# Five gate blocks computed as seven products, early sums moved beside the attention, gates kept in DRAM

## The chip, the core and the metric

The kernel runs on one core of one Trainium2 chip, whose engines work side by side: TensorE (PE) multiplies matrices, VectorE (DVE) and ScalarE (ACT) do elementwise work, GpSimd (POOL) and SyncE (SP) mostly issue DMA transfers here. The metric is the time of one execution on the device in microseconds (us), as the median of several runs.

## What is computed

One layer of an encoder with 512 tokens and a width of 2048, all in float32:

```python
def reference(x, ...):                       # x: (1, 512, 2048)
    h = rmsnorm(x, norm_mix)
    proj = h @ w_in                          # 2048 x 8704
    qa, ka, va, qb, kb, vb, ga, gb = split(proj)
    out_a = window_attention(rope(rmsnorm(qa)), rope(rmsnorm(ka)), va, sink)
    out_b = neighbourhood_attention(rmsnorm(qb), rmsnorm(kb), vb, rpb)
    merged = (sigmoid(ga) * (out_a @ w_branch_a)
              + sigmoid(gb) * (out_b @ w_branch_b))
    x = x + merged @ w_out
    u = conv3(rmsnorm(x) @ w_up)             # up: 2048 x 11264, gate and value
    gate, val = split(u)
    return x + (silu(gate) * val) @ w_down   # down: 5632 x 2048
```

`ga` and `gb`, the gates, are 2048 wide each. The factors of h by rows (1/rms of a token) and by columns (norm_mix) are applied apart: the acts carry norm_mix, and results are multiplied by the row factor.

## The kernel before

Matrices are worked off in **units**: a unit is 1024 columns by 128 rows of weights, for instance two k-tiles of 128 rows by 512 columns (512 KB). Activations lie transposed, 128 features by 512 tokens in a tile. A float32 product is made of three matmuls, hi x hi, hi x lo and lo x hi: ACT casts the weights to a rounded `hi` (L155), DVE subtracts (`lo`, L156). A plain unit has 8 pairs of k-tile and output tile, so 24 matmuls of 512 columns each, all recorded at L78, the line of `mm`; all SP transfers are recorded at L75. `hi` and `lo` have two buffers each, the raw weights three.

In the order of the program the stages are: the projections with both attentions between them (72 units: k and v of A 8, q_a in two halves of 8, and for each of four pairs of heads of B 4 units of v_b and 8 of q_b and k_b; the attention of a pair runs behind the projections that follow), gate blocks 0 and 1, gate block 2 (called the third gate block below; the attention's pools are closed at its start), branch A (out_a @ w_branch_a in four blocks), gate block 3, four gate blocks of B, branch B, `out` (w_out in four blocks), `up` and `down`.

Only `up` and `down` are worked in **products**: by the scheme of Strassen and Winograd a 2 x 2 block product needs seven products instead of eight. The price is sums of weights and of activations. Of the weights, a unit has four sums (L574 of 512 elements, L577 and L578 of 256 each); those of the activations are made by `forms` (sums at L627 to L630, casts at L638, subtractions at L639). Casting the weights is L597, subtracting L598; the combination of the seven results stands at L743 to L760. A product unit is 42 matmuls of 256 columns.

For part of the units of `up`, the sums are made **early** and kept in DRAM (`make_early`): f is loaded, added and stored by GpSimd (L581) in four of five units between the third gate block and `out`, 76 in all; `up` then loads sums in place of adding.

The order of instructions within an engine is the Tile scheduler's. It starts from the order of the program; `keep` holds an instruction in program order. The queue of an engine runs strictly in that order. Lines which the steps use: heads are squared, reduced, normed and rotated (L303 to L328), transposed and split (L335, L228, L229); v is transposed at L384. In the attention scores get bias and mask (L504, L508), are reduced (L449), raised (L456), scaled (L466), transposed and split (L477, L481, L482). A gate leaves PSUM by a multiplication with the row factor (L785) and the sigmoid (L786). `split_parts` (L832, L833) splits the attention's outputs for the branches. `wst_ctx.close()` ends the pool of plain weights and opens the one of products ("w"), before in the last unit of `out`.

Of the kernel before, what the change touches and what calls it, by code (L numbers as in the profile page):

```python
# [11 lines left out]
F32 = mybir.dt.float32  # L12
F32R = mybir.dt.float32r
AF = mybir.ActivationFunctionType
ALU = mybir.AluOpType
# [24 lines left out]
def trunk_kernel(  # L40
# [24 lines left out]
    def slot(dt=F32):  # L65
        return big.tile([P, S], dt, tag="s", name="s", bufs=N_SLOTS)
# [48 lines left out]

    steps, units, queue = [], [], deque()
    at = {"load": 0, "sums": 0, "prep": 0, "use": 0}

    def step(layout, w, cols, acts, evac, k0=0, nk=KD, before=None, pre=None, post=None, rate=RATE):

        width = sum(n for _, n in cols)
        kpb = 1024 // width
        steps.append(partial(
            run_step, layout, kpb, width, nk, acts, evac, before, pre, post, rate))
        for k in range(0, nk, kpb):
            units.append(Plain(w, k0 + k, kpb, cols))

# [34 lines left out]
    def prep_to(n, between=(), **kw):  # L162

        for u in units[at["prep"]:n + 1]:
            if hasattr(u, "first") and u.first > ffn.get("limit", -1):
# [378 lines left out]

    ffn, products_, early, made = {}, [], deque(), deque()
    keep = tc.keep_in_program_order

    class Product:
# [10 lines left out]
        def ready(self, phase, n):  # L559
            return "f" in ffn and not early and self.first <= n  # L560

# [9 lines left out]
        def sums(self):  # L571
            if not self.made:
# [5 lines left out]
                keep(nc.vector.tensor_tensor(f[:, 6], f[:, 5], f[:, 1], ALU.add))  # L578

        def store(self):  # L580
            nc.gpsimd.dma_start(self.kept, self.f[:, 3:])  # L581
            self.made = True
# [20 lines left out]
    def make_early():  # L603


        if "f" not in ffn or not early:
            return
        made.append(0)
        if len(made) % 5 == 0:
            return  # L610
        n = len(made) - len(made) // 5 - 1
        for move, i in (("store", n - 2), ("sums", n - 1), ("load", n)):
            if 0 <= i < len(early):
                getattr(early[i], move)()
        if n - 2 == len(early) - 1:
            early.clear()

# [57 lines left out]
    class Tiles:  # L675


        def __init__(self, w, first):
            self.w, self.first = w, first

        def ready(self, phase, n):
            return "f" in ffn and not early and self.first <= n

# [7 lines left out]
        def prep(self, *between):  # L691
            hi, lo = (
                ffn["w"].tile(
                    [P, 1024 + 32], F32R, tag=f"{half}a{self.first % 2}",
                    name="w" + half, bufs=1)[:, 16:16 + 1024].rearrange(
                        "p (f n) -> p f n", f=4)
                for half in "hl")
            keep(nc.scalar.copy(hi, self.f))
            keep(nc.vector.tensor_tensor(lo, self.f, hi.bitcast(F32), ALU.subtract))
            self.hi, self.lo = (v.rearrange("p (b c) n -> p b (c n)", b=2) for v in (hi, lo))  # L700
            for work in between:
                work()

    def tiles_by_halves(w, pairs, acts, evac, before=None, after=None):
# [28 lines left out]
        for i in range(n):  # L733
            units.append(Tiles(w[pairs[i]], len(units)))
            products_.append(units[-1])
# [39 lines left out]

    ra, sg, merged, oa, ob = {}, {}, [None] * KD, [], []

    def gates(c0, base, evac, **kw):
        step("f", w_in, [(c0 + base * P, 512)], hT, lambda m, ps: evac(base + m, ps), **kw)

    def branch(w, m0, acts, evac, **kw):
        step("f", w, [(m0 * P, 512)], acts, lambda m, ps: evac(m0 + m, ps), nk=8, **kw)

    def sigmoid(m, ps, s):
# [3 lines left out]
    half = {}  # L788

    def slot_of(tag):  # L790

        if tag is None:
            return slot()
        if tag not in half:
            half[tag] = quad(tag)
            return half[tag][:, 0]
        return half.pop(tag)[:, 1]

    def gate_first(store):
        def evac(m, ps):  # L800
            tag = ({2: "u", 3: "o"} if store is sg else {2: "a"}).get(m // 4)
            store[m] = slot_of(tag)
            sigmoid(m, ps, store[m])
        return evac

    def gate_after(m, ps):
        s = scratch()
        sigmoid(m, ps, s)
        nc.vector.tensor_tensor(ra[m], ra[m], s, ALU.mult)

    def evac_a(m, ps):
        if m < 12:
            nc.vector.tensor_tensor(ra[m], ps, ra[m], ALU.mult)
        else:
            ra[m] = slot()
            nc.scalar.copy(ra[m], ps)

    def evac_b(m, ps):
        s, r = sg[m], ra[m]
        nc.vector.tensor_tensor(s, ps, s, ALU.mult)  # L820
        nc.vector.tensor_tensor(r, r, s, ALU.add)
        merged[m] = split(r)

# [10 lines left out]

    def split_out(dst, src):
        for o in src:
            dst.append(load_parts(o))
            split_parts(*dst[-1])

    for blk in range(2):  # L840
        gates(C_GA, blk * 4, gate_first(ra))

    def load_a():
        end_attention()
        oa.extend(load_parts(o) for o in out_a)

    def before_gate(kb):
        if kb >= 4:
            for parts in oa[2 * kb - 8:2 * kb - 6]:
                split_parts(*parts)  # L850

    gates(C_GA, 8, gate_first(ra), pre=load_a, before=before_gate)
    for blk in range(4):
        branch(w_branch_a, blk * 4, oa, evac_a)
    gates(C_GA, 12, gate_after)

    def before_b(kb):
        if kb >= 4:
            split_out(ob, out_b[2 * kb - 8:2 * kb - 6])
# [21 lines left out]
    def project_out(n):  # L881
# [5 lines left out]
        def before(kb):  # L887
# [5 lines left out]
            if n == 3 and kb in (2, 4, 6, 7):  # L893
                form_pair({2: 2, 4: 3, 6: 4, 7: 5}[kb])
            if n == 3 and kb == 7:
                wst_ctx.close()
                ffn["w"] = ctx.enter_context(tc.tile_pool(name="w", bufs=2, reuse_waits="tile"))
                ffn["limit"] = at["use"] + 1

# [6 lines left out]
        def post():  # L906
            if n == 3:
                ffn["limit"] = len(units)
                prep_to(at["use"] + 1)
                form_pair(6)  # L910
                form_pair(7)

        step("f", w_out, [(n * 512, 512)], merged, evac, pre=pre, before=before, post=post)

# [213 lines left out]
```

## Time and profile before

| | |
|---|---|
| median of 3 runs | 2505.21 us (2503.06 to 2506.1) |
| the profiled execution: its time | 2502.81 us |
| its span in the trace | 2501.0 us |
| attention and gate blocks 0 and 1 | 0 to 580 us |
| third gate block | 580 to 624 us |
| branches and other gates | 624 to 1017 us |
| `out` | 1017 to 1191 us |
| `up` | 1193 to 2030 us |
| `down` | 2030 to 2501 us |

How to read what follows: a row of instructions gives line, engine, operation, output <- input with shape and count, then the busy time and the mean ns of one, then the idle time of the engine just before them and what ended it. A row of stretches gives, for a stretch of the execution, the busy time of each engine. Busy PE is no proof that PE runs at its full pace, as matmuls overlap; the number of matmuls in a full stretch gives their pace.

### The profile page before, as it was taken

What the parts mean: (1) busy time and instruction counts of PE and PEld (TensorE: products, weight loads), DVE (VectorE), ACT (ScalarE), POOL (GpSimd) and SP (SyncE); (2) the same over time, 40 slices, a digit from 0 to 9 for tenths busy, and PEclk for the clock granted to TensorE, in tenths of its full rate; (3) what the DMA queues carried; (4) which work ended last, traced back from release to release, by engine and by line L of the source; (5) the groups of instructions that cost most, each with busy time, mean ns of one, the idle gap of its engine ahead of it and who ended that gap; (6) DMA issues with size and microseconds to landing.
All of it is one profiled execution on the core that took longest, in us unless ns stands there. A gap on an engine that the chain in (4) does not pass through costs nothing.

```text
span 2501.0 us, 43289 instructions
## 1 busy us (share of the span) xinstructions
PE 2471.2 (99%) x16726; PEld 2275.1 (91%) x16726; DVE 1763.1 (70%) x2643; ACT 1226.9 (49%) x1843; POOL 202.9 (8%) x234
## 2 busy tenths in 40 slices
PE   9999999999999999999999999999999999999998
PEld 7888888888888888888999999999999999999998
DVE  6566454644545457655788888888888878696897
ACT  5355544543222233233576666666666665453633
POOL 0100000000000000100011111111111101000000
PEclk9999999999999999999999999999999999999999
DMA  5322222337787887874488888888888897776753
GB/s 190 94 83 89 91 91 91 99 92 225 257 256 244 254 279 256 278 253 160 148 211 224 225 227 219 230 220 217 233 221 218 244 283 213 209 188 170 226 161 120
DMA packets 338064, 487.04 MB, mean 195 GB/s; under 512 B 27840, under 2 KB 251200, under 8 KB 337856
## 3 DMA queue, kind: packets, MB, share of 16 engines
q1 hardware_dynamic: 294912, 377.38, 48.7%
q0 software_dynamic: 38464, 98.49, 16.8%
q10 hardware_dynamic: 4480, 8.39, 0.9%
q8 instruction: 131, 2.15, 0.3%
q14 instruction: 77, 0.63, 0.1%
HBM read 354.22 MB, written 83.89 MB: 175 GB/s over the span
## 4 chain that ended last, share of the span: by engine, by line
PE 94%; DMA 2%; DVE 2%; ACT 1%; issue 0%; SPq 0%; DVEq 0%; ACTq 0%
PE mm L78 91%; PE tr L78 2%; DMA s<-act 1%; DMA f<-in_w_down 1%; PE tr L477 1%; DVE wl L598 1%; PE tr L335 0%; DVE s L970 0%; ACT wh L597 0%; SPq L75 0%; DVE t L743 0%; DVE u L1039 0%; PE tr L384 0%; ACT s L638 0%; DMA s<-in_x_t 0%
## 5 line engine op out<-in xcount | busy, mean ns | idle before, releaser
L78 PE MATMUL mm<-s,wh 128*128 128x256 f32 x7476 | 1245.9, 277 | 10.2 <-ACT wh L597 7.8
L78 PEld LDWEIGHTS mm<-s,wh 128*128 128x128 f32 x7476 | 1088.1, 188 | 11.8 <-ACT wh L597 9.0
L78 PE MATMUL mm<-s,wl 128*128 128x256 f32 x3738 | 939.4, 277 | 2.9 <-DVE wl L598 2.9
L78 PE MATMUL mm<-s,hi 128*128 128x512 f32 x2304 | 688.5, 390 | 0.9 <-DVE s L785 0.9
L597 ACT CAST wh<-f 128x1024 fp32r<-128x1024 f32 x486 | 446.5, 942 | 449.0 <-PE mm L78 315.6
L78 PEld LDWEIGHTS mm<-s,wl 128*128 128x128 f32 x3738 | 660.8, 188 | 3.7 <-DVE wl L598 3.6
L598 DVE TENSOR_TENSOR wl<-f,wh 128x1024 fp32r<-128x1024 f32 x486 | 517.1, 1088 | 144.2 <-ACT wh L597 143.8
L78 PEld LDWEIGHTS mm<-s,hi 128*128 128x128 f32 x2304 | 431.6, 188 | 89.3 <-ACT s L786 1.3
L156 DVE TENSOR_TENSOR lo<-raw,hi 128x1024 fp32r<-128x1024 f32 (+1 forms) x201 | 244.9, 1218 | 379.2 <-ACT hi L155 375.9
L155 ACT CAST hi<-raw 128x1024 fp32r<-128x1024 f32 (+1 forms) x201 | 210.6, 1048 | 537.9 <-PE mm L78 476.9
L78 PE MATMUL mm<-s,lo 128*128 128x512 f32 x1152 | 423.7, 390 | 0.0
L78 PE MATMUL mm<-hi,s 128*128 128x512 f32 x896 | 284.9, 394 | 5.4 <-ACT hi L155 5.4
L78 PEld LDWEIGHTS mm<-s,lo 128*128 128x128 f32 x1152 | 216.4, 188 | 44.1
L78 PEld LDWEIGHTS mm<-hi,s 128*128 128x128 f32 x896 | 167.7, 189 | 38.1 <-ACT hi L155 5.4
L78 PE MATMUL mm<-lo,s 128*128 128x512 f32 x448 | 176.2, 394 | 0.0
L574 DVE TENSOR_TENSOR f<-f 128x512 f32<-128x512 f32 x243 | 166.4, 685 | 0.0
L578 DVE TENSOR_TENSOR f<-f 128x256 f32<-128x256 f32 x243 | 103.2, 425 | 7.8
L577 DVE TENSOR_TENSOR f<-f 128x256 f32<-128x256 f32 x243 | 103.2, 425 | 7.7
L78 PEld LDWEIGHTS mm<-lo,s 128*128 128x128 f32 x448 | 84.6, 189 | 16.7
L939 POOL DMA_DIRECT2D o<-a x44 | 52.9, 1202 | 575.7 <-ACT a L938 430.9
L581 POOL DMA_DIRECT2D sums<-f x76 | 40.7, 535 | 571.7 <-DVE f L578 571.7
L936 ACT ACTIVATE o<-u,smalls 128x512 f32<-128x512 f32 x88 | 71.1, 808 | 9.9 <-DMA act<-o 7.0
(140 smaller groups left out, 1644.6 us busy)
## 6 DMA issues: line engine op xcount, KB each, us to landing
f<-in_w_up SPq DMA_DIRECT2D x252, 256.0 KB, 4.0
f<-in_w_up SPq DMA_DIRECT2D x428, 128.0 KB, 4.1
raw<-in_w_in SPq DMA_DIRECT2D x103, 512.0 KB, 3.9
o<-a POOLq DMA_DIRECT2D x88, 511.0 KB, 8.1
sums<-f POOLq DMA_DIRECT2D x76, 512.0 KB, 5.0
f<-sums SPq DMA_DIRECT2D x76, 512.0 KB, 5.2
s<-act SPq DMA_DIRECT2D x168, 128.0 KB, 3.9
f<-in_w_down SPq DMA_DIRECT2D x67, 256.0 KB, 3.3
```

The lines of the kernel that those rows point to most:

```text
L78: nc.tensor.matmul(o, l, r, start=start, stop=stop, skip_group_check=True)
L155: nc.scalar.copy(hi[:, c:c + n], self.raw[:, c:c + n])
L156: nc.vector.tensor_tensor(lo[:, c:c + n], self.raw[:, c:c + n], hi[:, c:c + n].bitcast(F32), ALU.subtract)
L477: nc.tensor.transpose(b[:, (j - j0) * P:(j - j0 + 1) * P], pr[j][:, off:off + P], ident)
L574: keep(nc.vector.tensor_tensor(f[:, 3:5], f[:, 2::-2], f[:, 6].unsqueeze(1).to_broadcast([P, 2, 256]), ALU.add))
L577: keep(nc.vector.tensor_tensor(f[:, 5], f[:, 4], f[:, 2], ALU.add))
L578: keep(nc.vector.tensor_tensor(f[:, 6], f[:, 5], f[:, 1], ALU.add))
L581: nc.gpsimd.dma_start(self.kept, self.f[:, 3:])
L597: keep(nc.scalar.copy(hi, f))
L598: keep(nc.vector.tensor_tensor(lo, f, hi.bitcast(F32), ALU.subtract))
L936: keep(nc.scalar.activation(self.o[:, m], u[:, m], AF.Identity, bias=cb[:, i:i + 1], scale=cw[:, i, 1:2]))
L939: keep(nc.gpsimd.dma_start(self.o[:, :, 1:], first[:, :, :S - 1], accum_op=ALU.add))
```

## The change

Gate blocks 3 to 7 (the last of A, the four of B) become products, eight units each. For that the activations h need sums too (`forms`, 56 tiles in slots): they are made in the third gate block, which stays plain. x is loaded once more from DRAM in pairs of tiles into `quad("a")`, which has two buffers, scaled by norm_mix on ACT, and summed, cast and subtracted. The pool of product weights is opened at the end of this block instead of at that of `out`.

All gates are computed ahead of the branches; the sigmoids of A and B are written to DRAM through GpSimd and loaded again two tiles at a time in the branches (`held`). Branches and `out` keep plain units, in the products' buffers (`Tiles`).

The early sums are no longer made in f buffers but in slots: of each unit's sums, 128 x 512 and 2 x 128 x 256, DVE makes the same three additions, at each unit from the tenth on in the attention and gate blocks 0 and 1 (77 groups), and 11 more in the branches, in quads. Per unit SP gets, in this order, two stores of the group added one unit before (256 KB each), then four loads of 128 KB.

```diff
+    def make_early():
-        made.append(0)
-        if len(made) % 5 == 0:
-            return
...
+        if added:
+            added.popleft().store()
+        if fetched:
+            fetched[0].add()
+            added.append(fetched.popleft())
+        if early and any(a <= at["use"] < b - 2 for a, b in windows):
+            early[0].fetch()
+            fetched.append(early.popleft())
...
+        def add(self):
+            a, b = self.early
+            c = quad("o")[:, 0] if "q" in ffn else slot()
+            c = c.rearrange("p (t n) -> p t n", t=2)
+            add = lambda *args: keep(nc.vector.tensor_tensor(*args, ALU.add))
+            add(c, a, b[:, 0].unsqueeze(1).to_broadcast([P, 2, 256]))
+            add(b[:, 0], c[:, 1], a[:, 0])
+            add(b[:, 1], b[:, 0], b[:, 1])
+            self.early = c, b
...
+        def store(self):
-            nc.gpsimd.dma_start(self.kept, self.f[:, 3:])
+            for i, o in enumerate(self.early):
+                dma(self.kept[:, 2 * i:2 * i + 2], o)
...
+    def load_x(j):
+        held[j] = quad("a")
+        dma(held[j], x_t[2 * j * P:(2 * j + 2) * P].rearrange("(a p) n -> p a n", p=P))
+    def form_h():
+        j = len(hf)
+        if j < KD // 2:
+            x = held.pop(j)
+            for i in range(2):
+                nc.scalar.activation(
+                    x[:, i], x[:, i], AF.Copy, scale=gmix[:, 2 * j + i:2 * j + i + 1])
+            hf.append(forms(x))
+            if j + 2 < KD // 2:
+                load_x(j + 2)
+    def before_forms(kb):
+        if kb != 6:
+            form_h()
+        if kb == 7:
+            wst_ctx.close()
+            ffn["w"] = ctx.enter_context(tc.tile_pool(name="w", bufs=2, reuse_waits="tile"))
...
     for blk in range(2):
-        gates(C_GA, blk * 4, gate_first(ra))
+        gates(blk * 4, gate_to_slot)
+    windows.append((9, len(units)))
+    gates(8, gate_to_quad, pre=pre_forms, before=before_forms, post=post_forms)
+    for blk in range(3, 8):
+        gate_products(
+            blk, kept=range(4) if blk == 3 else (1, 2),
+            before=parts_behind(out_a, oa, 1) if blk == 7 else None)
+    windows.append((len(units) + 2, len(units) + 64))
     for blk in range(4):
-        branch(w_branch_a, blk * 4, oa, evac_a)
-    gates(C_GA, 12, gate_after)
...
+        branch(w_branch_a, blk, oa, gate_a, evac_a, before=parts_behind(out_b, ob, 0))
     for blk in range(4):
-        gates(C_GB, blk * 4, gate_first(sg), before=before_b if blk == 3 else None)
-    for blk in range(4):
-        branch(w_branch_b, blk * 4, ob, evac_b)
+        branch(w_branch_b, blk, ob, gate_b, evac_b)
```

The new names of lines: casts and subtractions of plain weights are L162 and L163, the early additions L603, the scale of x L840, casts and subtractions of `forms` L665 and L666, its sums L654 to L657. Two places show how rows move.

First, the end of q_b and k_b of the third pair of heads, where the last four tiles are normed (`rq`, `qr`) while the attention of the pair of heads before ends (`pl`, `s`). DVE's queue there, before:

```order
L156 TENSOR_TENSOR lo_3747<-raw_3744,hi_3746 128x1024
L308 TENSOR_REDUCE rq_127<-t_3806 128x4
L229 TENSOR_TENSOR s_3676<-tr_3670,s_3675 128x512
L239 TENSOR_SCALAR rq_127<-rq_127 128x4
L482 TENSOR_TENSOR pl_3629<-tr_3625,ph_3628 128x256
L229 TENSOR_TENSOR s_3717<-tr_3711,s_3716 128x512
L313 TENSOR_TENSOR qr_3804<-qr_3804,rq_127 128x512
L308 TENSOR_REDUCE rq_127<-t_3813 128x4
```

and in the change, where `lo_4367` belongs to the first unit after it (v_b of the next pair), as `lo_3747` does above:

```order
L489 TENSOR_TENSOR pl_4215<-tr_4210,ph_4214 128x384
L320 TENSOR_TENSOR qr_4462<-qr_4462,rq_127 128x512
L236 TENSOR_TENSOR s_4284<-tr_4278,s_4283 128x512
L603 TENSOR_TENSOR s_4320<-s_4271,s_4272 128x512
L320 TENSOR_TENSOR qr_4469<-qr_4469,rq_127 128x512
L470 RECIPROCAL rc_4182<-sm_4145 128x4
L489 TENSOR_TENSOR pl_4225<-tr_4221,ph_4224 128x256
L603 TENSOR_TENSOR s_4272<-s_4320,s_4271 128x256
L236 TENSOR_TENSOR s_4337<-tr_4331,s_4336 128x512
L603 TENSOR_TENSOR s_4272<-s_4272 128x256
L163 TENSOR_TENSOR lo_4367<-raw_4364,hi_4366 128x1024
```

The three additions (L603) have come in, and `lo` of that unit, which stood ahead of the norms, has moved behind the last of them (`qr`) and behind the last subtraction of the tail. The same place in PE's queue, where the normed heads are transposed (`tr` from `qr`); before, between matmuls of the first two units behind (`hi_3746`, then `hi_3776` with `lo_3777`):

```order
L335 MATMUL tr_3936<-ident_91,qr_3811 128x2x4x16
L335 MATMUL tr_3984<-ident_91,qr_3811 128x2x4x16
L335 MATMUL tr_4024<-ident_91,qr_3811 128x2x4x16
L78 MATMUL mm_3833<-s_317,hi_3746 128x512
L78 MATMUL mm_3833<-s_316,lo_3747 128x512
L78 MATMUL mm_3832<-s_359,hi_3776 128x512
L78 MATMUL mm_3832<-s_360,hi_3776 128x512
L335 MATMUL tr_4064<-ident_91,qr_3804 128x2x4x16
L335 MATMUL tr_4064<-ident_91,qr_3811 128x2x4x16
L78 MATMUL mm_3832<-s_359,lo_3777 128x512
```

and in the change:

```order
L342 MATMUL tr_4792<-ident_91,qr_4448 128x2x4x16
L342 MATMUL tr_4792<-ident_91,qr_4455 128x2x4x16
L342 MATMUL tr_4792<-ident_91,qr_4462 128x2x4x16
L342 MATMUL tr_4792<-ident_91,qr_4469 128x2x4x16
L78 MATMUL mm_4476<-s_265,hi_4366 128x512
L78 MATMUL mm_4476<-s_266,hi_4366 128x512
```

All sixteen transposes, of which these are the last four, now stand ahead of the first matmul of the next unit.

Second, the third gate block. ACT's queue before held, after the eight casts of out_a, nothing but the next weights:

```order
L832 CAST s_5298<-s_5299 128x512
L832 CAST s_5301<-s_5302 128x512
L155 CAST hi_5310<-raw_5308 128x1024
L155 CAST hi_5344<-raw_5342 128x1024
L155 CAST hi_5381<-raw_5379 128x1024
```

In the change it holds, in one unit, the scales of a pair of x (`a_6396`) ahead of `hi`, and behind it the casts of the pair before (`a_6336`):

```order
L665 CAST s_6393<-a_6276 128x256
L665 CAST s_6435<-a_6336 128x256
L665 CAST s_6438<-a_6336 128x256
L840 ACTIVATE a_6396<-a_6396,gmix_86 128x512 x2
L162 CAST hi_6400<-raw_6398 128x1024
L665 CAST s_6441<-t_6431 128x256
L665 CAST s_6444<-t_6430 128x256
L665 CAST s_6447<-t_6430 128x256
L665 CAST s_6450<-t_6431 128x256
L665 CAST s_6453<-a_6336 128x256
```

DVE's queue in the change, for the same pair, with `lo` of the unit ahead of the sums (`t`):

```order
L163 TENSOR_TENSOR lo_6401<-raw_6398,hi_6400 128x1024
L654 TENSOR_TENSOR t_6430<-a_6336 128x512
L656 TENSOR_TENSOR t_6431<-t_6430,a_6336 128x256
L657 TENSOR_TENSOR t_6431<-t_6431,a_6336 128x256
L666 TENSOR_TENSOR s_6441<-t_6431,s_6441 128x256
L666 TENSOR_TENSOR s_6444<-t_6430,s_6444 128x256
L666 TENSOR_TENSOR s_6447<-t_6430,s_6447 128x256
L666 TENSOR_TENSOR s_6450<-t_6431,s_6450 128x256
L666 TENSOR_TENSOR s_6453<-a_6336,s_6453 128x256
```

and SP's queue, where each pair of x stands ahead of a unit's raw weights:

```order
L75 DMA a_6276<-in_x_t 128x2x512
L75 DMA raw_6278<-in_w_in 128x2x512
L75 DMA a_6336<-in_x_t 128x2x512
L75 DMA raw_6338<-in_w_in 128x2x512
L75 DMA a_6396<-in_x_t 128x2x512
L75 DMA raw_6398<-in_w_in 128x2x512
```

A pair takes the buffer of the pair but one before it: `a_6396` that of `a_6276`, whose last reader on DVE is the subtraction that writes `s_6393`. So three queues now carry the forms of h between the casts, subtractions and loads of the weights.

More of the change, by code (lines that the diff above doesn't have):

```diff
@@ L164, in prep_to @@
         for u in units[at["prep"]:n + 1]:
-            if hasattr(u, "first") and u.first > ffn.get("limit", -1):
+            if getattr(u, "first", -1) > ffn.get("limit", -1):
                 break
@@ L559, in ready @@
         def ready(self, phase, n):
-            return "f" in ffn and not early and self.first <= n
+            return "f" in ffn and self.first <= n
         def load(self):
@@ L681, in ready @@
         def ready(self, phase, n):
-            return "f" in ffn and not early and self.first <= n
+            return "f" in ffn and self.first <= n
         def load(self):
@@ L785, in sigmoid, with gates, gate @@
+    def gates(base, evac, **kw):
+        step("f", w_in, [(C_GA + base * P, 512)], hT, lambda m, ps: evac(base + m, ps), **kw)
+    def gate(m, ps, s):
         nc.vector.tensor_tensor(s, ps, rows["m"], ALU.mult)
         nc.scalar.activation(s, s, AF.Sigmoid)
[L788 to L804, printed above, removed]
@@ new lines, in parts_behind, with before, branch, before_unit @@
+    def parts_behind(src, dst, first):
+        def before(kb):
+            n = 2 * (kb - first)
+            if 0 <= n < 8:
+                dst.extend(load_parts(o) for o in src[n:n + 2])
+            for parts in dst[max(0, n - 2):max(0, n)]:
+                split_parts(*parts)
+        return before
+    def branch(w, blk, acts, gate_of, evac, before=None):
+        def before_unit(kb):
+            if before:
+                before(kb + 4 * blk - 8)
+            if kb == 1:
+                for j in range(2):
+                    held[j] = quad("a")
+                    dma(held[j], gate_of[2 * blk + j])
+        step("f", w, [(blk * 512, 512)], acts, lambda m, ps: evac(4 * blk + m, ps), nk=8,
+             before=before_unit, unit=Tiles)
@@ L894, in before @@
                 form_pair({2: 2, 4: 3, 6: 4, 7: 5}[kb])
[L895 to L898, printed above, removed]
         def evac(o, ps):
```

127 lines of the change are left out of this document (73 added, 54 removed).

## The prediction

> **What bounds the kernel now.** First the page's head and its chain of work that ended last, then the table of busy time by stretch, which shows each stage by itself (columns: stretch; length, then busy us and instructions of PE, of its weight loads, of DVE, ACT and POOL; granted clock; DMA share; GB/s).
>
> ```profile
> span 2501.0 us, 43289 instructions
> PE 2471.2 (99%) x16726; PEld 2275.1 (91%) x16726; DVE 1763.1 (70%) x2643; ACT 1226.9 (49%) x1843; POOL 202.9 (8%) x234
> PE 94%; DMA 2%; DVE 2%; ACT 1%; issue 0%; SPq 0%; DVEq 0%; ACTq 0%
> ...
> 170.00:180.00 10.00, 10.00 (x50) 8.68 (x49) 9.08 (x18) 6.61 (x10) 3.39 (x3) 1.00 0.17 52
> 180.00:190.00 10.00, 10.00 (x52) 8.39 (x51) 10.00 (x21) 2.87 (x5) 1.01 (x1) 1.00 0.31 97
> 200.00:300.00 100.00, 100.00 (x517) 86.12 (x516) 54.77 (x106) 51.32 (x108) 4.03 (x4) 1.00 0.28 89
> 580.00:624.00 44.00, 43.12 (x191) 35.69 (x191) 23.70 (x35) 14.18 (x20) 2.38 (x4) 1.00 0.68 213
> 755.00:930.00 175.00, 175.00 (x774) 144.91 (x773) 93.58 (x140) 48.16 (x57) 14.09 (x27) 1.00 0.80 256
> 1400.00:1700.00 300.00, 300.00 (x2635) 300.00 (x2634) 260.31 (x340) 195.98 (x254) 38.41 (x32) 1.00 0.85 225
> ```
>
> PE carries 94% of the chain and is full in nearly every stretch, so the time is PE's work plus the places where PE waits. Such places are few now. DVE's 55% at 200 to 300 us is a mean, though: at 180 to 190 us, where the heads of q_a are normed and rotated, DVE has nothing left (10.00 of 10.00). What is put on DVE in the attention must be judged there, not by the mean. The stretches also give PE's price: 175.00/774 = 0.226 us for a 512-wide matmul, 300.00/2635 = 0.114 us for a 256-wide one; one plain unit of 24 matmuls is 5.43 us.
>
> The waits show how far ahead weights are prepared:
>
> ```profile
> ACT hi L155 <- PE mm L78: 476.9, 137, 6.2
> PE mm L78 <- ACT wh L698: 2.5, 1, 2.5
> ```
>
> 137 times the cast of the next weights stood waiting for PE to release a buffer: the lead of the preparation is already used up, about one unit. A late DVE has some 5 us of cover and no more.
>
> **Term 1, PE's work.** Gate blocks 3 to 7 go from 192 matmuls of 512 columns each to 336 of 256. Removed: 5 x 192 x 0.226 = 217 us. Added: 5 x 336 x 0.114 = 191 us. Net **-26**. Their sums, casts and combinations are what `up` does already; at 1400 to 1700 us DVE needs 260 of 300 us beside a full PE, and that row is the cover. The last gate block also splits out_a; by my count of its instructions DVE has about 39 us there for 38 us of PE, at most 1 to 3 us.
>
> **Term 2, early sums beside the attention.** Rows of instructions (last figures: busy, mean ns of one):
>
> ```profile
> L574 DVE TENSOR_TENSOR f<-f 128x512 f32<-128x512 f32 x243 | 166.4, 685 | 0.0
> L578 DVE TENSOR_TENSOR f<-f 128x256 f32<-128x256 f32 x243 | 103.2, 425 | 7.8
> L577 DVE TENSOR_TENSOR f<-f 128x256 f32<-128x256 f32 x243 | 103.2, 425 | 7.7
> L156 DVE TENSOR_TENSOR lo<-raw,hi 128x1024 fp32r<-128x1024 f32 (+1 forms) x201 | 244.9, 1218 | 379.2 <-ACT hi L155 375.9
> ...
> L482 DVE TENSOR_TENSOR pl<-tr,ph 128x256 fp32r<-128x256 f32 (+1 forms) x64 | 30.3, 486 | 24.4 <-ACT ph L481 24.4
> L449 DVE TENSOR_REDUCE nm<-p 128x1 f32<-128x256 f32 (+1 forms) x64 | 29.0, 478 | 0.2
> L313 DVE TENSOR_TENSOR qr<-qr,rq 128x512 f32<-128x512 f32 (+1 forms) x28 | 18.1, 648 | 5.5 <-POOL rq L240 5.5
> L308 DVE TENSOR_REDUCE rq<-t 128x4 f32<-128x512 f32 (+1 forms) x28 | 17.8, 643 | 5.6 <-ACT t L306 5.6
> L508 DVE TENSOR_TENSOR p<-p,masks 128x256 f32<-128x256 f32 (+1 forms) x32 | 14.6, 484 | 0.0
> L504 DVE SCALAR_TENSOR_TENSOR p<-tr,bias 128x256 f32<-128x256 f32 (+1 forms) x32 | 14.4, 486 | 21.4 <-PE tr L78 11.9 <-DMA bias<-in_bias_b 9.3
> L229 DVE TENSOR_TENSOR s<-tr,s 128x512 fp32r<-128x512 f32 x18 | 11.9, 686 | 6.5 <-ACT s L228 6.4
> L239 DVE TENSOR_SCALAR rq<-rq 128x4 f32<-128x4 f32 (+1 forms) x28 | 4.4, 165 | 0.3
> ```
>
> 77 groups of three adds (0.685 + 2 x 0.425 = 1.535 us) make 118 us of new DVE work, each group kept in program order between two units' `lo`. The same sums leave later stages, where PE was full in any case, so that relief gains nothing. At 170 to 190 us DVE had 0.9 us free in 20, and about four groups (6.1 us) come in: at least 5 us must come out there.
>
> The order of the change tells more (section on the change): where a block of heads ends, no matmuls of projections are left between its transposes, and `lo` of the next unit stands behind the whole tail. Take the end of q_b and k_b of the third pair of heads. After the scores that `p_4158` needs, DVE has until `lo_4367`: three each of L504, L508 and L449 (4.3), two L308 and four L313 (3.9), four L482 (1.9), two L229 (1.4), four small ones (0.7), the three adds (1.5) and `lo` (1.2), in all 15.0 us. PE has, by width, 34 transposes of 128 (0.057 each, in proportion to 0.226 for 512), 9 matmuls of 384, 9 of 256 and 5 of 512, about 5.6 us, and two that need only `hi` (0.5). The gap is 15.0 - 6.1 = 8.9; some instructions overlap their neighbours a little, so I take 8. Counted likewise: 12.5 at the end of q_a's second half, 8 at the end of the fourth pair, 5.4 ahead of gate block 1, 4.4 and 2.7 around the first two pairs, 1.1 in q_a's first half; sum **42**. Bounds: with 0.08 us overlapped for each instruction 27, and 20 if matmuls fall between the transposes of one tail after all; above, if the losses chain through ACT, whose casts of the tail stand before the next `hi`, 55. I take **+38**, near the count by rows.
>
> SP's order changes too: per unit it now holds raw weights, two stores that wait for the adds of two units back, four fetches. The next raw load is queued behind a store that waits for DVE. Cover: that load is issued a unit ahead (5.4 us) and lands in 3.9 (row below). I add nothing; without the cover, 3.9 us at each of the six larger ones, 23, which the upper end holds. The rate rises by 1.05 MB in each unit, from 89 GB/s to about 250; at 755 to 930 us 256 GB/s went beside a PE busy for 175.00 of 175.00 us, so rate is not a limit.
>
> **Term 3, the third gate block, which now also forms h.** It took 44 us (580 to 624), 8 units at 5.43. The change puts a loop through four queues into each unit: x pair j+2 may be loaded only when the last subtraction on pair j has freed its quad; the scales of that pair stand ahead of the next unit's `hi` on ACT; `lo` stands ahead of the next sums on DVE; the casts wait for the sums.
>
> ```profile
> L155 ACT CAST hi<-raw 128x1024 fp32r<-128x1024 f32 (+1 forms) x201 | 210.6, 1048 | 537.9 <-PE mm L78 476.9
> ...
> L231 ACT ACTIVATE s<-s,gmix 128x512 fp32r<-128x512 f32 x16 | 10.9, 714 | 2.8 <-DMA s<-in_x_t 2.8
> L639 DVE TENSOR_TENSOR s<-a,s 128x256 fp32r<-128x256 f32 x24 | 9.2, 419 | 0.0
> L638 ACT CAST s<-t 128x256 fp32r<-128x256 f32 x32 | 10.6, 402 | 17.2 <-DVE t L630 17.2
> L627 DVE TENSOR_TENSOR t<-a 128x512 f32<-128x512 f32 x8 | 5.5, 684 | 0.0
> L629 DVE TENSOR_TENSOR t<-t,a 128x256 f32<-128x256 f32 x8 | 3.4, 423 | 0.2
> L630 DVE TENSOR_TENSOR t<-t,a 128x256 f32<-128x256 f32 x8 | 3.4, 422 | 0.2
> ...
> raw<-in_w_in SPq DMA_DIRECT2D x103, 512.0 KB, 3.9
> o<-a POOLq DMA_DIRECT2D x88, 511.0 KB, 8.1
> ...
> s<-in_x_t SPq DMA_DIRECT2D x32, 256.0 KB, 6.2
> out_a<-o ACTq DMA_DIRECT2D x8, 256.0 KB, 2.0
> ```
>
> One turn: load 3.9 (same size and queue as raw), two scales 1.43, `hi` 1.05, `lo` 1.22, three sums 1.53, five casts 2.01, the last subtraction 0.42: 11.55 us. PE has 5.43, so 6.1 us are lost per turn. Five full turns, 30.6, and the first load 3.9: **+34**. With the shortest landing of the rows (2.0) 23; with 6.2, that of x at the crowded start, 48. The Trainium skill, "DMA: Bandwidth & Descriptors", section "Anatomy of one DMA", gives 2 us fixed plus bytes at 436 GB/s, as an estimate 3.2 us for 512 KB, which would make this term 30; the trace's 3.9 is for the same size and decides.
>
> Before the first product the pool of the next weights is opened, and a single wait for the first weights arises, as at L698 now (2.5); that one goes, since `out` changes no pool any more. Net nothing; 3 us either way. The rest I cost at nothing too. Gates go to DRAM through GpSimd (8% busy) and come back, 1 MB for a branch block, loaded ahead of the second of its four units, 16 us before they are used; `o<-a`, the slowest row of that size, lands in 8.1. If one came late it would hold the evacuation, not PE, until the PSUM banks run out. The 16 branch and 16 `out` units keep their PE work and their cast and subtraction, in other buffers.
>
> **Sum.** The profiled execution took 2502.8 us; 2502.8 - 26 + 38 + 34 = 2549. The median of the runs is 2.4 above it, so I predict **2550**.
>
> **Rivals.**
> (a) *The stock of prepared weights hides the lags*: DVE and the loop fall behind only as long as `hi`/`lo` stand ready, and the gain of the products comes through: 2505 - 26 = 2479, faster. It decides if the stock outlasts 12.5 us (2.3 units) at the worst tail and 34 us (6.3 units) in the loop. Against it: the casts already waited 137 times for PE to free a buffer, a stock of one unit. 55% DVE at 200 to 300 us speaks for it.
> (b) *Only one place bites.* If the scheduler's tails lie under matmuls after all, 2505 - 26 + 34 = 2513; if x lands early enough for the loop to open, 2505 - 26 + 38 = 2517. With one unit of stock taken off at each spot (12 + 29 left) 2520.
> (c) *Both at their upper ends, and the clock falls*: 2505 - 26 + 55 + 48 = 2582. The clock:
>
> ```profile
> 1192.00:1196.00 4.00, 2.88 (x13) 2.88 (x14) 4.00 (x7) 4.00 (x7) 0.06 (x1) 0.65 0.16 66
> 1196.00:1200.00 4.00, 4.00 (x34) 4.00 (x33) 3.86 (x6) 2.07 (x4) 0.00 (x0) 0.92 0.76 225
> ```
>
> After the wait of L698 the granted clock was 0.65, then 0.92 for 4 us each, a loss of 1.4 + 0.3 us. Six of them at 1.7 are 10 us, so the forecast would become 2560 and this case 2592; in the loop PE is not the bound and nothing is lost. [...]
> (d) *The products don't pay*: if 256-wide matmuls come slower for want of DVE, term 1 is 0 and the sum 2505 + 38 + 34 = 2577.
>
> **How the numbers follow.** Forecast (both places near my terms, with or without the clock; 2525 to 2565) 0.52; (a) 0.12; (b) 0.20; (c) 0.11; (d) 0.05. The range leaves out (a) and half of (c): 2508 to 2582. About 0.2%, 5 us, is what a measurement can tell from no change. Faster 0.12 is (a); within 0.2% 0.05, the low edge of (b); slower 0.83.
>
> **What would show it.** Right: PE idle some 8 us, waiting for `lo` (L163), at the ends of q_a and of the third and fourth pair; eight units of the third gate block some 11.5 us apart, with PE waiting for `hi` or `lo` and ACT's scale (L840) for x; the five product blocks near 38 us each with PE full. Wrong: those blocks clearly above 40 us, a full PE at the tails, or raw weights arriving late in every unit, which would make SP's new order the bound.

## The result, and the profile after

The changed kernel takes **2619.4 us** (median of 4 runs, 2618.8 to 2623.9) against 2505.2: ratio 1.0461, 95% interval 1.0443 to 1.0479. It is 114 us slower; forecast were 45 us, and the range ended at 2582. The profiled execution took 2619.3 us.

The head and the chain of work that ended last, from the page of the changed kernel:

```profile
span 2617.5 us, 45852 instructions
PE 2500.9 (96%) x17446; PEld 2308.6 (88%) x17446; DVE 1901.5 (73%) x2903; ACT 1286.5 (49%) x1956; POOL 173.7 (7%) x178
PE 74%; DMA 9%; DVE 8%; ACT 3%; SPq 2%; issue 2%; DVEq 0%; ACTq 0%
PE mm L78 73%; SPq L75 2%; DMA sums<-u 2%; DMA s<-in_w_up 2%; DMA raw<-in_w_in 2%; DVE s L603 2%; DMA s<-act 1%; DMA a<-in_x_t 1%; ACT hi L162 1%; PE tr L78 1%; DVE lo L163 1%; DMA u<-in_w_up 1%; DVE s L666 1%; DVE nm L456 1%; DVE wl L628 0%
```

PE's share of the chain fell from 94% to 74%. DMA, DVE and SP's queue (SPq) took its place. Where, the stretches tell; first two of before, then of after (columns as in the prediction: length, then busy us and instructions of PE, weight loads, DVE, ACT, POOL; clock, DMA share, GB/s):

```profile
60.00:581.00 521.00, 520.12 (x2569) 441.26 (x2567) 282.86 (x511) 242.45 (x459) 28.26 (x24) 1.00 0.32 97
581.00:624.60 43.60, 43.60 (x193) 36.10 (x194) 23.49 (x34) 13.41 (x20) 2.79 (x5) 1.00 0.67 208
```

```profile
60.00:658.00 598.00, 554.24 (x2570) 451.51 (x2568) 383.15 (x742) 238.42 (x458) 32.16 (x30) 0.97 0.68 215
658.00:736.00 78.00, 55.79 (x192) 42.82 (x192) 39.07 (x83) 36.00 (x80) 1.61 (x3) 0.85 0.39 141
736.00:928.00 192.00, 191.87 (x1682) 191.79 (x1683) 161.18 (x214) 96.25 (x119) 4.79 (x9) 1.00 0.54 166
...
977.00:1046.00 69.00, 49.16 (x176) 37.71 (x175) 30.07 (x46) 12.40 (x16) 0.00 (x0) 0.85 0.71 224
```

From 60 us on, the same 2570 matmuls or so of the attention and gate blocks 0 and 1 take 598 us instead of 521: **+77**. The 192 of the third gate block take 78 instead of 43.6: **+34.4**. The five product blocks take 192 us for 1680 matmuls, full, against 217 for the plain ones: **-25**. And in branch A PE does 176 matmuls of 512 columns in 69 us, which is 39.8 us of work at 0.226: **+29**. The sum, 115, is the whole result to 1 us.

What the engines wait for from 60 us to the start of the third gate block (waits: who, for whom, us in total, times, longest); the cast of raw weights before, then in the change with SP's own queue:

```profile
ACT hi L155 <- PE mm L78: 165.0, 54, 6.2
```

```profile
ACT hi L162 <- DMA raw<-in_w_in: 195.9, 46, 10.7
...
SPq L75 <- DVE s L603: 208.9, 115, 16.4
```

Before, the weights were ready and the cast waited for a free buffer. Now the cast waits for the weights, and SP, which fetches them, waits 208.9 us for the early additions (L603). The chain at the end of the third pair of heads, the place that the prediction worked out (start, us, what):

```profile
444.43 0.33 DVE s L603
...
445.27 0.43 DVE s L603
...
445.72 0.33 SPq L75
...
446.10 0.42 SPq L75
...
446.57 0.45 SPq L75
...
447.07 0.43 SPq L75
...
447.54 0.48 SPq L75
...
448.12 6.22 DMA raw<-in_w_in
...
454.36 1.05 ACT hi L162
...
455.46 14.72 PE mm L78 x56
```

DVE's tail ends at 445.7. From 433.0 to 447.5 us PE has some 6 us of work by the widths of its matmuls, so it loses some 8 us of the 14.5, as forecast. Behind the tail come the second of two stores and four loads, 0.33 to 0.48 us each to issue, and only then the raw weights of the next unit, which need 6.2 us more; PE waits again, until 455.46. The prediction had the first part and not the second.

### The profile page after: what moved, and what is told of

Same layout as the page of the kernel before. It is cut to its first block, busy times and chain, and to the rows that moved or that the text cites. A ratio compares the mean times of both kernels' runs of the same rounds, so it can differ in the third digit from the quotient of the medians.

```text
span 2617.5 us, 45852 instructions
## 1 busy us (share of the span) xinstructions
PE 2500.9 (96%) x17446; PEld 2308.6 (88%) x17446; DVE 1901.5 (73%) x2903; ACT 1286.5 (49%) x1956; POOL 173.7 (7%) x178
## 4 chain that ended last, share of the span: by engine, by line
PE 74%; DMA 9%; DVE 8%; ACT 3%; SPq 2%; issue 2%; DVEq 0%; ACTq 0%
PE mm L78 73%; SPq L75 2%; DMA sums<-u 2%; DMA s<-in_w_up 2%; DMA raw<-in_w_in 2%; DVE s L603 2%; DMA s<-act 1%; DMA a<-in_x_t 1%; ACT hi L162 1%; PE tr L78 1%; DVE lo L163 1%; DMA u<-in_w_up 1%; DVE s L666 1%; DVE nm L456 1%; DVE wl L628 0%
## 5 line engine op out<-in xcount | busy, mean ns | idle before, releaser
L78 PE MATMUL mm<-s,wh 128*128 128x256 f32 (+1 forms) x9620 | 1737.0, 290 | 24.3 <-ACT wh L726 16.1
L78 PEld LDWEIGHTS mm<-s,wh 128*128 128x128 f32 x9620 | 1445.1, 188 | 69.0 <-ACT wh L726 18.0
L78 PE MATMUL mm<-s,wl 128*128 128x256 f32 (+1 forms) x4810 | 1261.4, 289 | 7.8 <-DVE wl L727 5.4
L627 ACT CAST wh<-f 128x1024 fp32r<-128x1024 f32 (+1 forms) x566 | 520.3, 942 | 530.1 <-PE mm L78 381.5
L628 DVE TENSOR_TENSOR wl<-f,wh 128x1024 fp32r<-128x1024 f32 (+1 forms) x566 | 602.6, 1088 | 173.5 <-ACT wh L627 161.1
L163 DVE TENSOR_TENSOR lo<-raw,hi 128x1024 fp32r<-128x1024 f32 (+1 forms) x97 | 117.7, 1214 | 187.8 <-ACT hi L162 187.4
L727 DVE TENSOR_TENSOR wl<-f,wh 128x1024 fp32r<-128x1024 f32 x85 | 104.0, 1224 | 182.0 <-ACT wh L726 181.9
L78 PE MATMUL mm<-s,hi 128*128 128x512 f32 x640 | 203.2, 419 | 32.4 <-ACT hi L162 31.4
L162 ACT CAST hi<-raw 128x1024 fp32r<-128x1024 f32 (+1 forms) x97 | 100.8, 1039 | 268.0 <-DMA raw<-in_w_in 197.7
L726 ACT CAST wh<-f 128x1024 fp32r<-128x1024 f32 x85 | 89.3, 1051 | 235.1 <-PE mm L78 221.5
L78 PEld LDWEIGHTS mm<-s,hi 128*128 128x128 f32 x640 | 127.6, 203 | 65.0 <-ACT hi L162 37.1
L78 PE MATMUL mm<-s,lo 128*128 128x512 f32 x320 | 118.8, 409 | 2.1 <-DVE lo L163 1.8
L603 DVE TENSOR_TENSOR s<-s 128x256 f32<-128x256 f32 (+1 forms) x231 | 117.7, 509 | 2.4
L1008 POOL DMA_DIRECT2D o<-a x44 | 52.9, 1203 | 581.1 <-ACT a L1007 471.2
```

The costliest lines, as they stand in the source:

```text
L78: nc.tensor.matmul(o, l, r, start=start, stop=stop, skip_group_check=True)
L162: nc.scalar.copy(hi[:, c:c + n], self.raw[:, c:c + n])
L163: nc.vector.tensor_tensor(lo[:, c:c + n], self.raw[:, c:c + n], hi[:, c:c + n].bitcast(F32), ALU.subtract)
L603: add = lambda *args: keep(nc.vector.tensor_tensor(*args, ALU.add))
L627: keep(nc.scalar.copy(hi, f))
L628: keep(nc.vector.tensor_tensor(lo, f, hi.bitcast(F32), ALU.subtract))
```

## The experiments

All times stand beside runs of the kernel before on the same chip, which took 2503 to 2507 us. Runs 1 to 12 are one execution each. In runs that change nothing ahead of the block its start still moves by up to 4.6 us (658.0 in the change, 658.7 to 660.8 in runs 4, 5 and 8; 620.9 and 625.5 in runs 6 and 10), so smaller gains are not told apart. "The block" is the third gate block; its start is that of its first matmul (581.0 us before, 658.0 in the change).

**1. Stores of the attention from GpSimd.**

```diff
-                dma(self.kept[:, 2 * i:2 * i + 2], o)
+                if "q" in ffn:
+                    dma(self.kept[:, 2 * i:2 * i + 2], o)
+                else:
+                    nc.gpsimd.dma_start(self.kept[:, 2 * i:2 * i + 2], o)
```

> The early stores beside the attention are issued by GpSimd instead of SP; loads, additions and their order on DVE stay. Theory A (SP: raw weights are queued behind stores that wait for DVE, and arrive late): the third gate block starts 35 to 40 us earlier than in the change (at about 620 us instead of 658), the cast of raw weights waits under 80 us for their load instead of 196, total about 2580. Rival B (DVE's added work and the tails without matmuls are the loss by themselves): the block still starts after 645 us, total above 2605. Rival C (the rate of the transfers is the limit): nothing changes, as the bytes are the same.

2582.0 us; the block starts at 619.0, and the casts wait 53 us for raw weights instead of 196. The bytes are the same, so the rate of the transfers is not what made this half of the loss: 39 us of the attention's 77 hung on SP's order. The other 38 us stayed.

**2. No early sums.**

```diff
-    windows.append((9, len(units)))
...
-    windows.append((len(units) + 2, len(units) + 64))
```

> No early sums at all (both stretches of them left out); all products add for themselves. The loss up to the third gate block (77 us) and that in branch A (29 us) should both be gone, so that this block starts near 580 us as before. What the early sums are worth shows in the product blocks and in up: by DVE's work there (842 of 837 us of PE in up, and about 38 of 38 in the gate blocks) 5 to 40 us are lost. Total 2520 to 2555, so below the change; if the early sums earn what they cost, it is above 2619.

2540.3 us. The block starts at 581.1, to 0.1 us as before, and branch A loses nothing. From its first matmul to its last `up` takes 867.8 us against 841.1 in the change: 27 us are what 88 early groups earn there. They cost 77 + 29 = 106.

**3. Four buffers for x.**

```diff
-        held[j] = quad("a")
+        held[j] = quad("au"[j % 2])
...
-            if j + 2 < KD // 2:
-                load_x(j + 2)
+            if j + 4 < KD // 2:
+                load_x(j + 4)
```

> In the third gate block x is loaded into four buffers (two of the tag a, two of the tag u) four pairs ahead instead of two. Theory: the load of 3.8 us leaves the loop and a unit takes about 7.3 us instead of 11.2 (hi, lo, three sums, five casts and two scales remain in a chain), the block 52 to 56 us instead of 79, total 2593 to 2597. Rival (ACT and DVE, not the load, set the pitch): 11 us a unit as before, total 2619.

2611.6 us, a miss for both theories: the block takes 65.9 us instead of 78. One unit took 8.0 us, three still 11 and one 7.2, only then PE's 5.4 came. More buffers for x alone shorten the loop for a few units and don't open it.

**4. No second stretch.**

```diff
-    windows.append((len(units) + 2, len(units) + 64))
```

> The second stretch of early sums, 11 groups in branch A, is left out; up adds these sums itself. Theory (a closed loop over two pairs of quads: store 5.6 to 7 us, then load 2.4, then the additions, with the cast weights behind them on DVE): branch A loses nothing, up nothing that shows, total 2589 to 2593. Rival (branch A is late for other reasons: out_b is loaded and split there, gates are loaded): the loss of 29 us stays, total above 2612.

2592.6 us. Branch A loses nothing. In its stretch PE is full, 306 matmuls for 176:

```profile
977.00:1046.00 69.00, 69.00 (x306) 57.14 (x305) 32.27 (x39) 19.52 (x23) 0.00 (x0) 1.00 0.51 172
```

**5. Scales of x in program order.**

```diff
-                nc.scalar.activation(
-                    x[:, i], x[:, i], AF.Copy, scale=gmix[:, 2 * j + i:2 * j + i + 1])
+                keep(nc.scalar.activation(
+                    x[:, i], x[:, i], AF.Copy, scale=gmix[:, 2 * j + i:2 * j + i + 1]))
```

> In the third gate block the scales of x are held in program order, so that each pair is scaled directly ahead of its own forms, a unit later than the scheduler put it; two buffers as in the change. Theory A (the loop closes through the scales, which stand ahead of the next hi on ACT): 6 to 7 us a unit, the block near 50 us instead of 79, total 2590. Rival B (it closes a second time through SP, where the raw weights of the next unit are queued behind a load of x that waits for the last subtraction): hi then waits for raw, which takes 4 to 5 us to land, the pitch stays at 10 to 11.5 us, total 2610 to 2620.

2625.4 us: rival B, 5 us above its range; the block takes 81.7 us. The chain shows one turn of this run:

```profile
689.52 4.30 DMA raw<-in_w_in
...
694.85 1.33 ACT a L840 x2
...
698.41 0.41 ACT s L665
...
701.06 4.63 DMA raw<-in_w_in
705.77 1.04 ACT hi L162
```

`hi` now stands ahead of the scales, but raw takes the place of x in the chain: on SP it is queued behind a load of x that waits for DVE's last subtraction. The turn stays at 11.5 to 12 us.

**6. Raw weights one unit earlier.**

```diff
-            self.load(pieces)
+            if not hasattr(self, "raw"):
+                self.load(pieces)
...
             at["prep"] += 1
+            if at["use"] >= 9 and any(isinstance(v, Plain) for v in units[at["prep"]:at["prep"] + 1]):
+                units[at["prep"]].load()
```

> From the tenth unit on the raw weights are loaded one unit earlier (they have three buffers); stores and fetches stay on SP, with as many issues. Theory A (raw is late because it waits behind stores, which wait for DVE): the third gate block starts at 615 to 625 us, as with the stores on GpSimd (619), and the casts wait little for raw; total about 2580 (the block itself still loops through the scales, 11 us a unit). Rival B (SP's time to issue seven transfers in a unit is what counts): start after 645 us, total above 2605.

2559.0 us, better than theory A. The block starts at 620.9, 37 us earlier, with every issue still on SP: the lost lead was the cause, not the number of issues. The casts still wait 105.5 us for raw weights, which theory A had not expected. And the block itself now loses 8 us instead of 34, since each raw load is issued a unit ahead of its use; the scheduler then groups the scales by two pairs. What is left in the attention, 40 us, lies almost wholly at six tails, by an estimate from the widths of the matmuls there (0.226 us for 512 columns, and 5% more, as that stage took before) some 11, 6, 6, 8, 9 and 5 us. The chain at the tail of the third pair still runs through SP in this run:

```profile
431.32 0.43 DVE s L606
...
434.41 5.37 DMA raw<-in_w_in
439.81 1.05 ACT hi L163
```

L606 are the additions here. They end, the stores and loads are issued, and raw lands 8 us behind them. The tails of q_a's second half and of the fourth pair show the same: there one unit of lead is not enough.

**7. Stores on GpSimd (as in 1) and no additions.** The kernel leaves the early sums of the attention out and stores the loaded weights in their place.

```diff
+            if "q" not in ffn:
+                self.early = a, b
+                return
             add(c, a, b[:, 0].unsqueeze(1).to_broadcast([P, 2, 256]))
```

> Stores on GpSimd as in the first run, and the three additions of each early group beside the attention are left out (what is stored are the loaded weights, so the sums are not computed); all transfers stay. Theory A (what is left there, 38 us over the kernel before, is DVE's added work): the third gate block starts at 580 to 588 us, total 2543 to 2552. Rival B (the transfers themselves: rate, landing times, slots held longer): it starts after 605 us, total above 2568.

2560.6 us, between the theories: the block starts at 597.9, so 21 of the 38 us went and 17 stayed. The chain at a tail of this run shows why this run is no clean test:

```profile
409.62 1.00 POOL rq L247
410.62 0.55 POOL sums L617
411.17 1.43 issue
412.60 0.04 POOLq L617
...
412.65 1.04 POOL rq L247
```

GpSimd makes a step of the norms of the heads (`rq`), and its stores, which wait too, now stand between those; here that costs 2.0 us. Part of the wait had moved from SP to GpSimd; how much of the 17 us, this run does not say.

**8. The second stretch at every other unit.**

```diff
-        if early and any(a <= at["use"] < b - 2 for a, b in windows):
+        if early and any(a <= at["use"] < b - 2 for a, b in windows) and (
+                "q" not in ffn or at["use"] % 2):
```

> The 11 groups of the second stretch are fetched at every other unit instead of every one, so a quad has two units to be stored before it is loaded again. Theory A (closed loop of store, load and additions over two quads): the loop of about 11 us fits into two units of 10.9, branch A loses 0 to 4 us instead of 29, total 2590 to 2595. Rival B (each group costs what it costs, wherever it lies, by DVE and SP): the 29 us are spread over twice as many units, total 2612 to 2620.

2591.6 us: as many groups, 11, and branch A loses nothing. The loop over the quads was the cause, not the work.

**9. Raw weights ahead and no additions** (the edits of 6 and of `add` in 7; the early sums of the attention are left out again).

> Raw weights a unit earlier, as in the sixth run (2559; the third gate block started at 621 us, 40 us more loss than before, nearly all of it at six tails), and the three additions beside the attention left out, so those sums are not computed; stores and loads stay on SP. Theory A (the 40 us at the tails are DVE's added work and what its place in the queue does to the next lo): the block starts at 581 to 588 us, total 2518 to 2528. Rival B (loads that wait at the tails for buffers, and SP behind them, make the loss without any addition): it starts at 605 to 620 us, total above 2540.

2531.1 us, a little above theory A: the block starts at 594.0, 27 us earlier than in 6 and 13 later than before. All transfers are still made, 242 GB/s in this stage, so their rate alone costs at most these 13. Where they are lost, the chains tell. At one place, 338 to 352 us, some 6 us are lost to loads: with the additions gone SP waits for buffers that the attention's outputs still hold, and raw is late behind that wait:

```profile
SPq L75 <- DMA out_a<-o: 59.4, 5, 21.6
```

At three other places (196 to 203, 408 to 420 and 488 to 499 us) the chain has no transfer: it runs through DVE's and ACT's work on the tail to `hi`, which stands behind that work on ACT.

**10 to 14. The remedies together.** Raw weights ahead, scales kept, every other unit in the second stretch (the edits of 6, 5 and 8):

> Three remedies together: raw weights a unit earlier, the scales of x in program order, the second stretch at every other unit. If the mechanisms are separate, their gains add: from the run with raw weights ahead (2559) branch A takes 28 off, and the third gate block, which still lost 8 there, loses 2 to 5: total 2525 to 2531, what is left over the kernel before being the tails of the attention (about 40) less 26 of PE's work. If the remedies only shift the wait (a rival), above 2540.

2535.1 us, a few above theory: branch A loses nothing, which takes 30 us off against 6, but the block starts 4.6 us later; keeping the scales gave nothing (the block loses 7.6).

In addition, no group fetched in the three units ahead of a tail and in its first, then in the five ahead:

```diff
+        tails = (30, 45, 50, 60, 72, 79)
-        if early and any(a <= at["use"] < b - 2 for a, b in windows):
+        if early and any(a <= at["use"] < b - 2 for a, b in windows) and (
+                at["use"] % 2 if "q" in ffn else not any(
+                    t - 3 <= at["use"] <= t for t in tails)):
```

> As the run with three remedies, and no early group is fetched in the three units ahead of a tail of the attention and in its first (24 of 77 groups; 31 instead of 11 go to every other unit of the branches and out, so some 80 groups of 88 are still made). Theory A (the tails are late since DVE carries the additions and slots of fetches there): the loss up to the third gate block falls from 57 us (raw weights ahead) to 20 to 30, total 2490 to 2505. Rival B (the tails are late by their own work in the changed order): it stays above 45, total above 2515.

> The same with five units ahead of each tail left out (36 to 40 groups stay beside the attention, up adds some ten to fifteen more by itself). Theory A: the attention is as before (loss of 17 to 22 us up to the third gate block), up 3 to 6 us longer, total 2485 to 2500. Rival B: no better than with three units left out, above 2515.

2496.2 and 2496.1 us; the block starts at 589.0 and 588.1, 7 to 8 us later than before. Leaving out three units is enough. (The 57 us of the expectation are 48 by the block's start and length in run 6: 40 and 8.) What the block itself still loses, 8 us, was then tried with the edit of 3, with the version of three units beside it for its interval; in this version the second stretch also ends eight units earlier, with 26 groups in it instead of 30:

> The run with three units left out, and x in four buffers loaded four pairs ahead; the second stretch ends eight units earlier. Theory: of the 8 us that the third gate block still loses, the waits for raw weights behind a load of x (three of 4.5 to 4.9 us in the chain) go; 2 to 4 us are left; the start of up loses 2 to 4 us less. Total 2486 to 2492, 12 to 18 below the kernel before. Rival (the chain of DVE and ACT in that block is the limit in any case): total as with three units left out, 2496.

> The version with three units left out once more, for its interval against the kernel before: 2494 to 2498 against 2503 to 2507, ratio 0.995 to 0.998.

With x in four buffers 2490.1 us (5 runs), ratio 0.9947, interval 0.9935 to 0.996; with two, 2496.0 (7 runs), 0.997, 0.9959 to 0.9981. The block loses 4.7 us instead of 7.6, which is half of the 6 us between them; where the rest lies is not shown. Both beat the kernel before, by 0.5% and 0.3%, and the first is **129 us faster than the change** as it was made.

## Why the prediction was wrong

**Direction and two of three places were right, two steps failed.** It said slower (0.83), for the attention and the third gate block; branch A it left out.

**Term 1, PE's work (-26): right.** 192 us for 1680 matmuls against 217. Rival (d) is out.

**Term 2, the additions (+38): right in size.** With the stores off SP (run 1) the attention loses 38 us more than before. By the same estimate from widths as in run 6, the six tails lose some 12, 5, 6, 8, 8 and 5 us there; counted were 12.5, 4.4, 2.7, 8, 8 and 5.4. The chain of run 1 at the tail of the third pair is DVE's tail, and behind it ACT's, which the prediction had in its upper bound:

```profile
425.55 1.92 ACT p L473 x4
427.47 0.47 ACT o L497
427.94 0.96 ACT hi L162
428.92 1.24 DVE lo L163
```

Run 6 leaves nearly as much, 40 us, but at its three largest tails the chain runs through SP and raw weights, so that its agreement with the count is luck. Runs 7 and 9 leave out the additions, and 21 and 27 us go; but with them goes also SP's or GpSimd's wait for them, so no run separates DVE's added work from what its lateness does to the queues. 13 to 17 us stay without any addition.

**Term 2, SP's queue: the first step that failed.** The prediction wrote: "Cover: that load is issued a unit ahead (5.4 us) and lands in 3.9 (row below). I add nothing; without the cover, 3.9 us at each of the six larger ones, 23". Measured are 37 to 39 us (runs 6 and 1). The cover is a unit ahead in the *program*. Where DVE is late the load stands behind stores whose additions are late with it, so it is issued with no lead left. Beside run 1, at the same matmuls of the projections, the change loses some 22 of its 39 us at the six tails, much as the 23 of a lost cover. The other 17 lie between the tails, where the prediction named no lag. The first place is at 108 to 119 us, where one unit takes 10.8 us instead of 6.4: DVE norms and rotates heads of q_a, and SP's queue stands for 7 us at the two stores (start, us, what):

```profile
103.13 7.03 SPq L75 DMA_DIRECT2D sums<-s  x2
...
112.18 0.38 SPq L75 DMA_DIRECT2D raw<-in_w_in  x1
```

The prediction's own sign of this, raw weights that arrive late, came: 46 waits, 195.9 us. Its remark that the upper end holds the 23 was wrong too, as that end, 55, lies only 17 above the term. The Trainium skill, "DMA: Bandwidth & Descriptors", section "Anatomy of one DMA", says that a wait for a semaphore happens on the issuing sequencer, ahead of the dispatch; the 208.9 us of SP agree. Its section "Issuing engines are not separate DMA queues" expects of a second issuing engine only the time of issuing; run 1, which moved two waiting stores, gained 37 us, and run 6 as much in the attention with every issue still on SP, so here the measurement decides otherwise.

**Term 3, the third gate block (+34): right, 34.4 measured.** Five turns of 10.9 to 11.5 us lose 29 of the 30.6 forecast; the rest came at the second unit (1.7) and the last (4.0), and not as the first load's 3.9. One turn was put at 11.55 us; the chain has it:

```profile
697.84 3.79 DMA a<-in_x_t
...
701.71 1.29 ACT a L840 x2
...
703.04 1.05 ACT hi L162
704.12 1.23 DVE lo L163
705.34 0.61 DVE t L654
705.98 0.44 DVE t L656
...
706.90 0.41 ACT s L665
...
708.68 0.45 DVE s L666 x2
709.13 3.62 DMA a<-in_x_t
```

11.3 us from load to load. But the link that the prediction named (scales ahead of `hi` on ACT) is only one of two that close it. Run 5 takes it out and gains nothing; run 6 takes out the other, raw behind x on SP, and the loss falls to 8. Run 10 has both edits and also loses 8, so it hangs on the place of raw.

**Branch A: the second step that failed, and the one left out.** "The rest I cost at nothing too ... The 16 branch and 16 `out` units keep their PE work and their cast and subtraction, in other buffers." The same branches also got 11 early groups, in quads with two buffers, and these were not costed. The chain there:

```profile
1014.55 2.38 DMA u<-in_w_up
...
1017.13 0.35 DVE o L603
1017.48 5.49 DMA sums<-u
1022.98 0.33 SPq L75
...
1023.37 0.42 SPq L75
1023.84 2.19 DMA u<-in_w_up
```

Load, additions, a store of 5.5 us, and the next load into the same quad: a loop of the same kind as that of x, 9 to 12 us from load to load against 5.4 us of PE, over some six units. Runs 4 and 8 agree on it: 27 and 28 us. With SP's 39, these 29 are nearly the whole 69 us by which the forecast of 2550 was short.

**The clock.** Rival (c) priced it at 1.7 us for each of six tails. The rows above show 0.97 in the attention, 0.85 in the block and in branch A, where PE had stood for several us at a time, and 1.00 where it was full. In run 6 the attention had 0.99. What it cost by itself no run separates; it is part of the 77 us, by an estimate from 0.97 of 598 us at most some 18. One reading behind the rival was wrong: the wait at 1193 us before, ahead of its rows of the clock, is one for L597 (2.6 us), and L698's 2.5 us lies in `down`. In the change PE waits 0.9 us for the weights of the first product and 1.0 us for those of `up`, but there also 4.4 us for L270; `up` takes 841.1 us instead of 837.0.

By terms, the 77 split by run 1: 2505 - 25 + 38 + 39 + 34 + 29 = 2620.

## What to carry to other kernels

A queue that issues transfers runs in order: before a store goes into it, ask what it waits for, what load stands behind it, and whether that lead is still there when the producer is late; moving the load one unit earlier was worth 60 us here, 37 of them in the attention, and was still not enough at the largest tails. A buffer that is stored and loaded again is a loop (store, load, work), and its time must fit into the units between its two uses, which every other unit did and every unit did not. Work that is hidden in a stage by its mean share of an engine should be kept away from the places where that engine is full; leaving out 24 of 77 groups there, with more of them in the branches, took 39 us off.

## What had not been expected of the hardware

SP needs 0.33 to 0.48 us for the issue of one transfer (chain at the tail), so a unit with seven of them takes some 3 of its 5.4 us. And a load of 512 KB that lands in 3.9 us before took 5.0 in the median in the change and 6.2 at the tail, at 215 GB/s instead of 97 in that stage; a store of 256 KB of the same sums to DRAM took 2.9 in the median beside the attention and 5.6 in branch A.
